# Gate-weight splits placed behind a query tile's convolution, and one chunk's loads placed ahead of the next chunk's, at the seam of two scans

## The chip, the cores and the metric

The kernel runs on one core of one Trainium2 chip. The metric is device time in microseconds (us) for one execution. The profile's engines are PE (matrix products; PEld is its weight load), DVE (elementwise work), ACT (activation functions, scaled copies), POOL (elementwise work, some DMA issue) and SP (DMA issue only).

## The reference

One layer over 4096 rows of width 1024, float32. After an RMS norm, one projection yields the operands of two groups. Group B is a windowed attention. Group A, which matters here, is a matrix-memory recurrence in both directions over 32 chunks of 128 rows with 4 heads of 128:

```python
qk_a = jax.nn.silu(centred_depthwise_conv(qk_a, conv_w, conv_b))
q_a, k_a = jnp.split(qk_a.astype(jnp.float32), 2, axis=-1)
...
h_fwd = mlstm_one_direction(q_a, k_a, v_a, i_f, f_f)
h_bwd = jnp.flip(mlstm_one_direction(jnp.flip(q_a, 1), jnp.flip(k_a, 1), jnp.flip(v_a, 1),
                                     jnp.flip(i_b, 1), jnp.flip(f_b, 1)), 1)
h = jax.nn.sigmoid(o_a.astype(jnp.float32)).reshape(hs) * (h_fwd + h_bwd)
h = h * lax.rsqrt(jnp.mean(h * h, axis=-1, keepdims=True) + EPS)
...
y_a = h.reshape(bsz, seqlen, A_WIDTH) * jax.nn.silu(z_a.astype(jnp.float32))
```

Both groups are joined, projected, added to the input and normed again.

## The kernel before

Every large product is made of three products: each operand is split into a high part (a copy rounded to fp32r, made by ACT) and a low part (the rest, by a subtraction on DVE), and high x low, low x high and high x high are summed. A weight tile's split is the pair L104 (ACT) and L105 (DVE) in `load_split`. Each call of `wgroup` loads and splits one weight block of 1024 x 512 as four tiles j = 0..3, and each tile has two such pairs. `next_weights(0)`, `(1)` and `(2)` make `w3_0` (gate o), `w3_1` (gate z) and `w3_2` (the attention's gate). In the trace their staging tiles are `w_0s`, `w_1s`, `w_2s`; in the listings of order they are `w3_1s2` and so on.

The work has three passes. `pass2` walks blocks b = 7 .. 0 of 512 rows backwards: value projection, then eight key and query tiles m (keys m = 4..7, then queries m = 0..3). Each tile is 24 matmuls (L879), an ACT copy to `U` (L883), a first tap on ACT (L895), four taps on DVE (L897), a tanh on ACT (L899), a closing product on DVE (L900) and a store to DRAM (`k_d`, `q_d`, L902). The four key tiles are transposed (`ktp`, PE L927) into a PSUM buffer of tag "b", which has two buffers; ACT casts it (L929) and DVE subtracts (L930) to give the split key `kt`. The "b" buffers go in turn to ktp 0, ktp 1, ktp 2, the product kv of chunk 3 and head 1, ktp 3, and so on. The products kv (L158 to L160) need `kt` and the weighted values (`wvr` on POOL and DVE L940, cast L942, low part L943); state C follows on DVE (L958) and goes to DRAM.

`pass3` walks chunks n = 0 .. 31 forwards. For each it computes the gates (`op`, `zp`, 24 matmuls each, L1176, in two PSUM buffers of tag "pj" that go in turn to op 0, zp 0, op 1, zp 1; the ACT tanh L1184 reads them out), loads query, key, value and state (`lq`, `lk`, `lv`, `lkf`, `CC`, L1084 and L1064) and two broadcast rows `E` and `W` (L1060), masks E on POOL (L1092), takes its exponential on ACT (L1096), multiplies the scores S (PE L1104) into it (DVE L1106), weighs the query (DVE L1118) and forms the numerators (L1128, L1129). Chunk 0's query comes from DRAM, where block 0's query tiles were stored.

PE's order is written out by hand. On the other engines a list scheduler orders the instructions by its own model of their times; `behind(c, ins)` holds what is issued within it until `ins` has been placed on that same engine. So the seam from pass2's block 0 to pass3's chunk 0 is where the key and query tiles, the splits of `w3_1` and `w3_2`, and the loads of chunks 0 and 1 share ACT, DVE and SP. The staging tiles of `w3_2` also occupy buffers that the loads of CC 0, E 1, W 1 and CC 1 take over: each of those loads waits for a split on DVE.

Of the kernel before, what the change touches and what calls it, by code (L numbers as in the profile page):

```python
# [823 lines left out]
def pass2(c):  # L824
    nc, tc, A = c.nc, c.tc, c.A
    with ExitStack() as es:
# [37 lines left out]
        def qkproj(b, m):  # L864
            w = wk_ if m >= 4 else wq
            h = m % 4
            cs = slice(h * 128, h * 128 + 128)
            parts = ((0, 258), (258, 514)) if b == 7 else ((0, 512),)
            R = {}

            def unit(lo, hi, k, j):
                if lo == 0 and k == 0 and j == 0:
                    R["U"] = wk.tile([128, 516], F32, tag="U", bufs=2, name=f"U{b}_{m}")
                if k == 0 and j == 0:
                    R["p"] = c.ps("pj", [128, 512], f"up{b}_{m}_{lo}")
                up, U = R["p"], R["U"]
                xh, xl = xv(b, k, lo, hi)
                a, x = ((1, xh), (0, xl), (0, xh))[j]
                nc.tensor.matmul(up[:, 0:hi - lo], w[k // 2][:, k % 2, a, cs], x, start=(k == 0 and j == 0),  # L879
                                 stop=(k == KT - 1 and j == 2))  # L880
                if k < KT - 1 or j < 2:
                    return
                nc.scalar.copy(U[:, lo:hi], up[:, 0:hi - lo])  # L883
                if hi != parts[-1][1]:
                    return
                if m == 4:
                    HL[b] = wk.tile([128, 8, 4], F32, tag="hl", bufs=2, name=f"hl{b}")
                if b == 7:
                    nc.gpsimd.memset(U[:, 514:516], 0.0)
                else:  # L890
                    nc.gpsimd.tensor_copy(U[:, 512:516], HL[b + 1][:, m, :])
                nc.gpsimd.tensor_copy(HL[b][:, m, :], U[:, 0:4])
                cm = (h + 4) if m >= 4 else h
                acc = wk.tile([128, 512], F32, tag="qk", bufs=4, name=f"qk{b}_{m}")
                c.ucopy = nc.scalar.activation(acc, U[:, 0:512], AF.Identity, bias=cb[:, cm:cm + 1], scale=cw[:, cm, 0:1])  # L895
                for t in range(1, 5):
                    nc.vector.scalar_tensor_tensor(acc, U[:, t:t + 512], cw[:, cm, t:t + 1], acc, ALU.mult, ALU.add)  # L897
                th = wk.tile([128, 512], F32, tag="th", bufs=1, name=f"th{b}_{m}")
                nc.scalar.activation(th, acc, AF.Tanh)  # L899
                nc.vector.scalar_tensor_tensor(acc, th, 1.0, acc, ALU.add, ALU.mult)  # L900
                dst = c.k_d if m >= 4 else c.q_d
                nc.sync.dma_start(dst[4 * b:4 * b + 4, :, h * 128:h * 128 + 128].rearrange("n p t -> p n t"),  # L902
                                  acc.rearrange("p (n t) -> p n t", n=4))
                if m >= 4:
                    KTS[b, h] = acc

            return [[[(lambda z=z: unit(*z)) for z in [(lo, hi, k, j) for j in range(3)]] for k in range(KT)]
                    for lo, hi in parts]

# [54 lines left out]
        for b in range(7, -1, -1):  # L964
            for pair in () if b == 7 else ((3, 2), (1, 0)):
                vu = [vproj(4 * b + i) for i in pair]
                for k in range(KT):
                    for u in vu[0][3 * k:3 * k + 3] + vu[1][3 * k:3 * k + 3]:
                        u()
            if b == 0:  # L970
                c.next_weights(0)
            for m in range(4, 8):
                for u in flat(qkproj(b, m)):
                    u()
                if b == 7 and m == 6:
                    gate4(c)
                    rnorm(c)
            n3 = 4 * b + 3
            if b < 7:
                weigh(n3)  # L980

            def kvp(n, hh):
                if hh == 0 and n > n3 - 3:
                    weigh(n - 1)
                kvmm(n, hh)

            fill = flat(qkproj(b, 0))
            if b == 7:
                fill.append(cost(0.0, lambda: (gate5(c), weigh(n3))))
            fill += flat(qkproj(b, 1)) + last_two(b)  # L990
            at = [((8, 16, 28, 38)[h] / 96, lambda h=h, b=b: ktp(b, h)) for h in range(NH)]
            if b == 0:
                at.append((37 / 96, lambda: c.next_weights(1)))
            at += [((34 + 62 * (4 * (n3 - n) + hh) / 16) / 96, lambda n=n, hh=hh: kvp(n, hh))
                   for n in range(n3, n3 - 4, -1) for hh in range(NH)]
            place(fill, at)
            if b == 0:
                with behind(c, c.ucopy):
                    c.next_weights(2)
                c.x0 = XB[0]  # L1000

# [34 lines left out]
def pass3(c):  # L1036
    nc, tc, A = c.nc, c.tc, c.A
    with ExitStack() as es:
# [7 lines left out]
        def load(n, names):  # L1046
            r = Ls.setdefault(n, {})
            for nm in names:
                if n >= NCH:
                    continue  # L1050
                if nm in "ew":
                    nme = f"{nm.upper()}{n}"
                    if nm == "e" and n > 1:
                        e = r[nm] = wk.tile([128, 2, NH, 128], F32, tag="e", bufs=3, name=nme)
                    else:
                        e = r[nm] = xtile(c, [128, 2, NH, 128], F32, nme)
                    for d in range(2):
                        m = (c.m_d if nm == "e" else c.w_d)[d, n if d == 0 else NCH - 1 - n].rearrange("h t -> (h t)")
                        with behind(c, TZ.get("x") if nm == "e" and n < 5 else None):
                            nc.sync.dma_start(e[:, d].rearrange("p h t -> p (h t)"), m.partition_broadcast(128))  # L1060
                    continue
                if nm == "cc":
                    t = CCs[n] = xtile(c, [128, NH, 2, 129], F32, f"CC{n}")
                    nc.sync.dma_start(t[:, :, 1, :], c.cb_d[n].rearrange("p (h d) -> p h d", h=NH))  # L1064
                    continue
                if nm == "x":
                    if n == 0:
                        for i in range(2):
                            XS[i] = lambda a, k, i=i: c.x0[k][:, a, 2 + i * 128:130 + i * 128]
                    elif n % 2 == 0:  # L1070
                        xs = []
                        for i in range(2):
                            XS[n + i] = lambda a, k, i=i, xs=xs: xs[k // 2][:, a, k % 2, i * 128:i * 128 + 128]
                        for kk in range(4):
                            t = xtile(c, [128, 2, 2, 256], F32R, f"xs{n}_{kk}")
                            for z in range(2):
                                TZ["x"] = nc.sync.dma_start(f32(t[:, z]), c.xT_d[z, 2 * kk:2 * kk + 2, :, n * 128:n * 128 + 256]
                                                  .rearrange("k p t -> p k t"))
                            xs.append(t)
                    continue  # L1080
                d = {"q": c.q_d, "k": c.k_d, "kf": c.kf_d, "v": c.v_d}[nm]
                w = 129 if nm in ("kf", "v") else 128
                t = r[nm] = wk.tile([128, NH, w], F32, tag="l" + nm, bufs=2, name=f"l{nm}{n}")
                nc.sync.dma_start(t.rearrange("p h d -> p (h d)"), d[n])  # L1084

        def decays(n):
            if n >= NCH:
                return
            e = Ls[n]["e"]
            for d in range(2):  # L1090
                sg = 1 if d == 0 else -1
                nc.gpsimd.affine_select(out=e[:, d], in_=e[:, d], compare_op=ALU.is_ge, fill=BIG, base=0,  # L1092
                                        pattern=[[0, NH], [sg, 128]], channel_multiplier=-sg)
                with behind(c, TZ.get(n - 1)):
                    for h in range(NH):
                        nc.scalar.activation(e[:, d, h, :], e[:, d, h, :], AF.Exp, bias=tmone(c, 0, d, h, n),  # L1096
                                             scale=-1.0)
# [96 lines left out]

        load(0, ("x", "k", "q", "e", "w", "cc", "v", "kf"))
        nc.gpsimd.memset(CCs[0][:, :, 0, :], 0.0)
        load(1, ("e", "w", "cc", "q", "k"))
        decays(0)
        weigh_q(0)
        load(1, ("v", "kf"))  # L1200
# [298 lines left out]
def body(nc, tc, A):  # L1499
    with ExitStack() as es:  # L1500
        c = setup(nc, tc, A, es)
        c.w3, c.w4, c.XR = [], [], {}

        def next_weights(i):
            c.w3.append(wgroup(c, (1536, 2048, 2560)[i], f"w3_{i}"))

        c.next_weights = next_weights
        with tc.manual_schedule(engines={mybir.EngineType.PE}):
# [47 lines left out]
```

## Time and profile before

| | us |
|---|---|
| runs shown: median of 3 | 2211.18 |
| runs shown: lowest, highest | 2203.68, 2211.2 |
| profiled execution, its own time | 2207.95 |
| its span (first to last instruction) | 2206.2 |
| seam, from the last key tiles to S of chunk 0 | about 1155 to 1206 of the span |

| engine | busy us in the span |
|---|---|
| PE | 2164.2 |
| DVE | 1411.1 |
| ACT | 1087.0 |
| POOL | 608.7 |

The mean granted PE clock is 0.994 of full speed. All times of the trace below count from the span's start. A row of the timeline gives start, length, engine, line, operation, output and inputs, and in brackets how long the engine was idle before it and who ended the idle time. The length of a row includes its completion, so the next row can start a little before it ends.

### The profile page before, as it was taken

How to read it: one execution, taken by the hardware profiler on the slowest of the kernel's cores; microseconds unless marked ns; L12 is line 12 of the kernel's file. 1: busy time of each engine (PE TensorE's matmuls, PEld its weight loads, DVE VectorE, ACT ScalarE, POOL GpSimd, SP SyncE). 2: the span in 40 equal slices, each digit the busy share in tenths (PEclk: the TensorE clock that was granted, in tenths of full speed). 3: DMA queues.
4: the chain of work that ended last, by engine and by line, in shares of the span. 5: the costliest groups of instructions: out<-in, count | busy, mean ns of one | idle time of the engine just before them, and what ended most of it. 6: DMA issues, size and time to landing. Idle time of an engine off the chain costs nothing.

```text
span 2206.2 us, 35191 instructions
## 1 busy us (share of the span) xinstructions
PE 2164.2 (98%) x12226; PEld 1877.9 (85%) x12226; DVE 1411.1 (64%) x3092; ACT 1087.0 (49%) x2712; POOL 608.7 (28%) x1059
## 2 busy tenths in 40 slices
PE   8999999999999999999999999999999999999998
PEld 7899999999797888888887888888888888888886
DVE  6677777787765566456667555555554443777776
ACT  6778888877643343334445444444443321333323
POOL 3456565662121211121112212112121111112222
PEclk9999999999999999999999999999999999999999
DMA  8654464432233452344266976777685998667774
GB/s 246 177 171 123 148 172 98 158 114 69 92 98 106 158 163 78 120 159 154 76 193 219 321 220 214 237 240 230 213 254 177 316 359 284 185 181 187 190 196 138
DMA packets 249134, 398.98 MB, mean 181 GB/s; under 512 B 21979, under 2 KB 128475, under 8 KB 248956
## 3 DMA queue, kind: packets, MB, share of 16 engines
q1 hardware_dynamic: 220544, 303.50, 45.5%
q0 software_dynamic: 28176, 92.96, 13.1%
q8 instruction: 96, 1.57, 0.3%
q14 instruction: 82, 0.67, 0.1%
q10 hardware_dynamic: 236, 0.27, 0.0%
HBM read 275.99 MB, written 120.67 MB: 180 GB/s over the span
## 4 chain that ended last, share of the span: by engine, by line
PE 78%; DMA 8%; issue 5%; DVE 5%; ACT 2%; POOL 2%; POOLq 0%; SPq 0%; DVEq 0%; ACTq 0%
PE up L879 15%; PE zp L1176 8%; PE op L1176 8%; PE qp L532 7%; PE v2p L852 7%; DMA xr<-x 5%; PE op L409 4%; PE tp L395 3%; PE sp L367 3%; PE zbp L158 3%; PE zbp L159 3%; PE zbp L160 3%; PE num L1129 3%; PE num L1128 3%; PE kp L468 2%
## 5 line engine op out<-in xcount | busy, mean ns | idle before, releaser
L879 PE MATMUL up<-xb,w 128*128 128x512 f32 x1344 | 338.3, 396 | 0.0
L1343 PE MATMUL o<-wo,yo 128*128 128x512 f32 (+1 forms) x1356 | 312.3, 392 | 0.0
L1343 PEld LDWEIGHTS o<-wo,yo 128*128 128x128 f32 x1356 | 253.2, 188 | 59.2
L879 PEld LDWEIGHTS up<-xb,w 128*128 128x128 f32 x1344 | 243.8, 188 | 47.0
L897 DVE SCALAR_TENSOR_TENSOR qk<-U,cw,qk 128x512 f32<-128x512 f32 x256 | 190.1, 754 | 93.6 <-ACT qk L895 88.8
L532 PE MATMUL qp<-xT,wqb 128*128 128x256 f32 x1536 | 246.2, 290 | 0.1
L532 PEld LDWEIGHTS qp<-xT,wqb 128*128 128x128 f32 x1536 | 217.2, 192 | 8.9 <-DVE xT L450 0.3
L1176 PE MATMUL op<-w,xs 128*128 128x512 f32 x720 | 202.4, 408 | 0.0
L1176 PE MATMUL zp<-w,xs 128*128 128x512 f32 x720 | 188.0, 402 | 0.7 <-DVE z L1186 0.7
L852 PE MATMUL v2p<-w,xb 128*128 128x512 f32 x672 | 158.0, 395 | 1.1 <-DMA xb<-xT_d 1.0
L1176 PEld LDWEIGHTS zp<-w,xs 128*128 128x128 f32 x720 | 130.9, 189 | 27.6 <-DVE z L1186 1.2
L852 PEld LDWEIGHTS v2p<-w,xb 128*128 128x128 f32 x672 | 126.0, 188 | 31.8 <-DMA xb<-xT_d 2.3
L370 DVE CUSTOM_DVE_ANT_0 s<-sp,G 128x320 f32<-128x320 f32 (+1 forms) x256 | 122.6, 480 | 44.3 <-PE sp L367 40.6
L398 DVE TENSOR_TENSOR pt<-tp,pt 128x512 fp32r<-128x512 f32 x188 | 129.2, 687 | 26.3 <-ACT pt L397 25.0
L379 ACT ACTIVATE s<-s,st 128x320 f32<-128x320 f32 (+1 forms) x256 | 139.7, 548 | 11.5 <-DVE st L377 11.1
L1176 PEld LDWEIGHTS op<-w,xs 128*128 128x128 f32 x720 | 126.8, 189 | 21.1
L397 ACT CAST pt<-tp 128x512 fp32r<-128x512 f32 x188 | 110.0, 586 | 63.5 <-PE tp L395 60.2
L1143 ACT ACTIVATE hs<-num,r 128x128 f32<-128x128 f32 x128 | 47.1, 368 | 175.4 <-DVE r L1140 129.3
L409 PE MATMUL op<-pt,v 128*128 128x512 f32 x376 | 121.8, 405 | 10.4 <-DVE ab L422 10.3
L367 PE MATMUL sp<-kk,q 128*128 128x320 f32 (+2 forms) x512 | 119.6, 315 | 4.3 <-DVE st L370 4.2
L395 PE MATMUL tp<-ident,s 128*128 128x128 f32 x752 | 114.2, 275 | 0.2 <-DVE pt L398 0.2
L1166 POOL DMA_DIRECT2D y_d<-ya x32 | 19.4, 607 | 326.0 <-ACT hs L1143 182.9
(274 smaller groups left out, 4529.9 us busy)
## 6 DMA issues: line engine op xcount, KB each, us to landing
xc<-xT_d SPq DMA_DIRECT2D x64, 512.0 KB, 8.2
xs<-xT_d SPq DMA_DIRECT2D x120, 256.0 KB, 6.4
xT_d<-xT POOLq DMA_DIRECT2D x104, 256.0 KB, 5.4
xb<-xT_d SPq DMA_DIRECT2D x48, 514.0 KB, 7.6
E<-m_d SPq DMA_DIRECT2D x64, 256.0 KB, 4.6
W<-w_d SPq DMA_DIRECT2D x64, 256.0 KB, 5.8
y<-y_d SPq DMA_DIRECT2D x32, 512.0 KB, 3.4
out<-xr POOLq DMA_DIRECT2D x31, 512.0 KB, 4.1
```

What stands on the lines that cost most here:

```text
L367: nc.tensor.matmul(sp[:, lo:hi], qt, kk[:, kv, z, col - 128 + lo:col - 128 + hi], start=(z == 0), stop=(z == 1))
L370: nc.vector.tensor_tensor_reduce(out=s[:, lo:hi], in0=sp[:, lo:hi], in1=bias[0][:, kv * 2 + m, lo - 64 * half:hi - 64 * half], op0=ALU.add ...
L379: nc.scalar.activation(ps[g][:, kept(g)], ps[g][:, kept(g)], AF.Exp, bias=ng[:, g:g + 1], accum_out=rs[:, g:g + 1])
L395: nc.tensor.transpose(tp[:, g * 128:(g + 1) * 128], ps[g][:, j * 128:(j + 1) * 128], c.ident)
L398: nc.vector.tensor_sub(pt[:, 1, :], tp, f32(pt[:, 0, :]))
L409: nc.tensor.matmul(op, vt, pt[:, z, :], start=(i == 0 and z == 0), stop=(i == len(js) - 1 and z == 1))
L532: nc.tensor.matmul(qp, wq[k // 2][:, k % 2, w, m * 128:m * 128 + 128], x[k], start=(k == 0 and j == 0), stop=(k == KT - 1 and j == 2))
L852: nc.tensor.matmul(vp, a, wv[k // 2][:, k % 2, m, :], start=(k == 0 and j == 0), stop=(k == KT - 1 and j == 2))
L879: nc.tensor.matmul(up[:, 0:hi - lo], w[k // 2][:, k % 2, a, cs], x, start=(k == 0 and j == 0), stop=(k == KT - 1 and j == 2))
L897: nc.vector.scalar_tensor_tensor(acc, U[:, t:t + 512], cw[:, cm, t:t + 1], acc, ALU.mult, ALU.add)
L1176: nc.tensor.matmul(P[nm], XS[n](a, k), w[:, m, :], start=(k == 0 and j == 0), stop=(k == KT - 1 and j == 2))
L1343: nc.tensor.matmul(p, a[:, z, k, :], w[k // 2][:, k % 2, m, lo:hi], start=k == 0 and z == 1, stop=k == 3 and z == 0 and m == 0)
```

## The change

There are two edits of the order of splits and two of the order of loads. No operation is added or removed.

```diff
-                nc.scalar.activation(th, acc, AF.Tanh)
-                nc.vector.scalar_tensor_tensor(acc, th, 1.0, acc, ALU.add, ALU.mult)
+                c.qth = nc.scalar.activation(th, acc, AF.Tanh)
+                c.qst = nc.vector.scalar_tensor_tensor(acc, th, 1.0, acc, ALU.add, ALU.mult)
...
                 if m >= 4:
                     KTS[b, h] = acc
+                    c.kth, c.kst = c.qth, c.qst
...
-                at.append((37 / 96, lambda: c.next_weights(1)))
+                def w1():
+                    c.next_weights(1, (0, 1))
+                    with behind(c, c.kth), behind(c, c.kst):
+                        c.next_weights(1, (2, 3))
+
+                at.append((37 / 96, w1))
...
-                with behind(c, c.ucopy):
+                with behind(c, c.qth), behind(c, c.qst):
                     c.next_weights(2)
...
-                nc.sync.dma_start(t.rearrange("p h d -> p (h d)"), d[n])
+                TZ[nm, n] = nc.sync.dma_start(t.rearrange("p h d -> p (h d)"), d[n])
...
-                with behind(c, TZ.get(n - 1)):
+                with behind(c, TZ.get(1 if n == 1 else n - 1)):
...
-        load(1, ("e", "w", "cc", "q", "k"))
+        with behind(c, TZ["q", 0]):
+            load(1, ("e", "w", "cc", "q", "k"))
...
-        def next_weights(i):
-            c.w3.append(wgroup(c, (1536, 2048, 2560)[i], f"w3_{i}"))
+        def next_weights(i, js=range(4)):
+            if len(c.w3) == i:
+                c.w3.append([])
+            c.w3[i] += wgroup(c, (1536, 2048, 2560)[i], f"w3_{i}", js=js)
```

In the listings below a tile's name carries its block and number: `qk0_7` is block 0, m = 7 (the last key tile), `qk0_0` the first query tile, `kt0_2` the split of key tile 2, `th0_3` the tanh of the last query tile.

DVE at the last key tile, before, from the splits of w3_1's third tile to the last key tile's closing product:

```order
L105 SCALAR_TENSOR_TENSOR w3_12_13229<-w3_1s2_13230,nw_88,w3_12_13229 128x512 x2
L897 SCALAR_TENSOR_TENSOR qk0_7_13104<-U0_7_13075,cw_7935,qk0_7_13104 128x512
L900 SCALAR_TENSOR_TENSOR qk0_6_13065<-th0_6_13071,qk0_6_13065 128x512
L930 TENSOR_TENSOR kt0_0_13136<-ktp0_0_13131,kt0_0_13136 128x512
L940 TENSOR_TENSOR wvr1_13299<-v2_1_12918,TM_8723 128x4x129
L105 SCALAR_TENSOR_TENSOR w3_13_13236<-w3_1s3_13237,nw_88,w3_13_13236 128x512
L897 SCALAR_TENSOR_TENSOR qk0_7_13104<-U0_7_13075,cw_7935,qk0_7_13104 128x512
L105 SCALAR_TENSOR_TENSOR w3_13_13236<-w3_1s3_13237,nw_88,w3_13_13236 128x512
L930 TENSOR_TENSOR kt0_1_13152<-ktp0_1_13147,kt0_1_13152 128x512
L897 SCALAR_TENSOR_TENSOR qk0_0_13166<-U0_0_13121,cw_7935,qk0_0_13166 128x512
L930 TENSOR_TENSOR kt0_2_13187<-ktp0_2_13182,kt0_2_13187 128x512
L900 SCALAR_TENSOR_TENSOR qk0_7_13104<-th0_7_13110,qk0_7_13104 128x512
```

The same place on DVE with the change, up to the split of key tile 2 (the two rows ahead of it are the first taps of qk0_7 and the closing product of qk0_6):

```order
L931 TENSOR_TENSOR kt0_0_13136<-ktp0_0_13131,kt0_0_13136 128x512
L897 SCALAR_TENSOR_TENSOR qk0_7_13104<-U0_7_13075,cw_7935,qk0_7_13104 128x512
L931 TENSOR_TENSOR kt0_1_13152<-ktp0_1_13147,kt0_1_13152 128x512
L897 SCALAR_TENSOR_TENSOR qk0_7_13104<-U0_7_13075,cw_7935,qk0_7_13104 128x512
L897 SCALAR_TENSOR_TENSOR qk0_0_13166<-U0_0_13121,cw_7935,qk0_0_13166 128x512
L900 SCALAR_TENSOR_TENSOR qk0_7_13104<-th0_7_13110,qk0_7_13104 128x512
L897 SCALAR_TENSOR_TENSOR qk0_0_13166<-U0_0_13121,cw_7935,qk0_0_13166 128x512
L105 SCALAR_TENSOR_TENSOR w3_12_13229<-w3_1s2_13230,nw_88,w3_12_13229 128x512 x2
L897 SCALAR_TENSOR_TENSOR qk0_0_13166<-U0_0_13121,cw_7935,qk0_0_13166 128x512
L105 SCALAR_TENSOR_TENSOR w3_13_13236<-w3_1s3_13237,nw_88,w3_13_13236 128x512 x2
L941 TENSOR_TENSOR wvr1_13299<-v2_1_12918,TM_8723 128x4x129
L931 TENSOR_TENSOR kt0_2_13187<-ktp0_2_13182,kt0_2_13187 128x512
```

The closing product of qk0_7 has moved ahead of the four splits, and kt0_2 has moved behind it, behind two more taps of qk0_0 and behind the splits; on ACT the cast of kt0_2 likewise stands behind the four splits now.

ACT from the last query tile's first tap to the tanh of op 0, before:

```order
L895 ACTIVATE qk0_3_13460<-U0_3_13396,cb_7936,cw_7935 128x512
L104 ACTIVATE w3_20_13470<-w3_2s0_13471,nw_88 128x512 x2
L104 ACTIVATE w3_21_13477<-w3_2s1_13478,nw_88 128x512 x2
L104 ACTIVATE w3_22_13484<-w3_2s2_13485,nw_88 128x512 x2
L104 ACTIVATE w3_23_13491<-w3_2s3_13492,nw_88 128x512 x2
L1096 ACTIVATE E0_13510<-E0_13510,TM_8723 128x128 x8
L899 ACTIVATE th0_3_13466<-qk0_3_13460 128x512
L1184 ACTIVATE o0_13600<-op0_13575 128x512
```

The same stretch of ACT with the change:

```order
L895 ACTIVATE qk0_3_13460<-U0_3_13396,cb_7936,cw_7935 128x512
L1102 ACTIVATE E0_13510<-E0_13510,TM_8723 128x128 x8
L899 ACTIVATE th0_3_13466<-qk0_3_13460 128x512
L104 ACTIVATE w3_20_13470<-w3_2s0_13471,nw_88 128x512 x2
L104 ACTIVATE w3_21_13477<-w3_2s1_13478,nw_88 128x512 x2
L104 ACTIVATE w3_22_13484<-w3_2s2_13485,nw_88 128x512 x2
L104 ACTIVATE w3_23_13491<-w3_2s3_13492,nw_88 128x512 x2
L1190 ACTIVATE o0_13600<-op0_13575 128x512
```

The exponentials of E 0 and th0_3 now stand ahead of the eight splits of w3_2, and the tanh of op 0 directly behind them.

SP's queue from the last query stores but one to chunk 0's key and query, before:

```order
L1060 DMA E0_13510<-m_d_72 128x512 x2
L902 DMA q_d_74<-qk0_2_13380 128x4x128
L1060 DMA W0_13513<-w_d_73 128x512 x2
L1064 DMA CC0_13516<-cb_d_78 128x4x129
L1060 DMA E1_13523<-m_d_72 128x512 x2
L1060 DMA W1_13526<-w_d_73 128x512 x2
L1064 DMA CC1_13529<-cb_d_78 128x4x129
L902 DMA q_d_74<-qk0_3_13460 128x4x128
L1084 DMA lk0_13506<-k_d_75 128x512
L1084 DMA lq0_13508<-q_d_74 128x512
```

The same stretch of SP's queue with the change:

```order
L1066 DMA E0_13510<-m_d_72 128x512
L902 DMA q_d_74<-qk0_2_13380 128x4x128
L1066 DMA E0_13510<-m_d_72 128x512
L1066 DMA W0_13513<-w_d_73 128x512 x2
L902 DMA q_d_74<-qk0_3_13460 128x4x128
L1070 DMA CC0_13516<-cb_d_78 128x4x129
L1090 DMA lk0_13506<-k_d_75 128x512
L1090 DMA lq0_13508<-q_d_74 128x512
L1090 DMA lv0_13518<-v_d_77 128x516
L1090 DMA lkf0_13520<-kf_d_76 128x516
L1066 DMA E1_13523<-m_d_72 128x512 x2
```

The store of the last query tile no longer has E 1, W 1 and CC 1 ahead of it; these five loads now follow chunk 0's four. PE's order is the same in both. On POOL only the wvr of chunk 1 moves, behind two small copies. Outside the seam the lists agree, but for a few rows of chunks 2 to 4 that change places with a neighbour.

## The prediction

> **What bounds the kernel now.** I read the page's busy times first, then PE's waits, then the chain that ended last through the seam. PE's row and its waits at the seam:
>
> ```profile
> PE 2164.2 (98%) x12226; PEld 1877.9 (85%) x12226; DVE 1411.1 (64%) x3092; ACT 1087.0 (49%) x2712; POOL 608.7 (28%) x1059
> ```
>
> ```profile
> PE S L1104 <- DMA lq<-q_d: 1.4, 1, 1.4
> PE ktp L927 <- DVE qk L900: 1.1, 1, 1.1
> ...
> PE kv L158 <- DVE kt L930: 0.4, 1, 0.4
> ```
>
> PE is busy for 98% of the span, so only what makes PE wait moves the time. (A wait's row gives total us, times, longest.) In the whole seam PE waits three times, 1.4 + 1.1 + 0.4 = 2.9 us together, 0.13% of the run. This is all that the change can win. The chain shows what ends the two larger waits:
>
> ```profile
> 1167.45 0.60 DVE kt L930
> 1168.05 0.61 DVE qk L900
> 1168.80 0.63 PE ktp L927 x4
> ...
> 1198.97 4.26 DMA q_d<-qk
> 1203.37 2.58 DMA lq<-q_d
> 1206.08 1.13 PE S L1104 x8
> ```
>
> The fourth key transposition waits for the last key tile's closing product on DVE. S of chunk 0 waits for the last query tile, which is stored (4.26 us) and loaded again (2.58 us).
>
> **The first edit: two tiles of w3_1 behind the last key tile.** Rows of PE, DVE, ACT and POOL at this place:
>
> ```profile
> 1160.60 3.03 PE L879 MATMUL up<-xb,w 128*128 128x512 f32 x12
> 1163.66 0.65 PE L927 MATMUL ktp<-ident,qk 128*128 128x128 f32 x4
> ...
> 1167.31 0.40 PE L879 MATMUL up<-xb,w 128*128 128x512 f32 x1
> ...
> 1169.96 0.28 PE L158 MATMUL kv<-wvh,kt 128*128 128x258 f32 x1
> ```
>
> ```profile
> 1157.87 1.54 DVE L897 SCALAR_TENSOR_TENSOR qk<-U,cw,qk 128x512 f32<-128x512 f32 x2 [0.17 <-POOL hl L892]
> 1159.46 1.41 DVE L105 SCALAR_TENSOR_TENSOR w<-w_1s,nw,w 128x512 fp32r<-128x512 f32 x2
> 1160.79 0.75 DVE L897 SCALAR_TENSOR_TENSOR qk<-U,cw,qk 128x512 f32<-128x512 f32 x1
> 1161.45 1.55 DVE L900 SCALAR_TENSOR_TENSOR qk<-th,qk 128x512 f32<-128x512 f32 x1
> 1162.92 0.68 DVE L930 TENSOR_TENSOR kt<-ktp,kt 128x512 fp32r<-128x512 f32 x1
> 1163.53 0.68 DVE L940 TENSOR_TENSOR wvr<-v,TM 128x516 f32<-128x516 f32 x1
> ...
> 1166.72 0.73 DVE L897 SCALAR_TENSOR_TENSOR qk<-U,cw,qk 128x512 f32<-128x512 f32 x1
> 1167.38 0.67 DVE L930 TENSOR_TENSOR kt<-ktp,kt 128x512 fp32r<-128x512 f32 x1
> ...
> 1173.08 0.68 DVE L940 TENSOR_TENSOR wvr<-v,TM 128x516 f32<-128x516 f32 x1
> ```
>
> ```profile
> 1163.04 0.58 ACT L883 COPY U<-up 128x512 f32<-128x512 f32 x1
> 1163.66 0.81 ACT L895 ACTIVATE qk<-U,cb,cw 128x512 f32<-128x512 f32 x1
> ```
>
> ```profile
> 1160.96 1.50 POOL L940 TENSOR_TENSOR wvr<-v,TM 128x516 f32<-128x516 f32 x1 [2.94 <-DVE w L105]
> ...
> 1171.86 2.82 POOL L940 TENSOR_TENSOR wvr<-v,TM 128x516 f32<-128x516 f32 x1 [5.62 <-PE kv L160]
> ```
>
> From start to start a tap (1166.72 to 1167.38) or a split (1.41 less one length of 0.75) costs DVE 0.66 us, a subtraction 0.60 (1162.92 to 1163.53), a closing product 0.61 by the chain.
>
> The fourth transposition needs more than the closing product. Its PSUM buffer is that of the third, so DVE must have subtracted kt0_2 as well. That PE really waits for such a buffer shows in the third one: it starts at 1163.66, 0.2 us after twelve matmuls of 0.23 us from 1160.60 are through, when kt0_0, whose buffer it takes, is done (1162.92 + 0.68). Before the change kt0_2 was done at 1168.05 and hid behind the closing product. Now it comes later:
>
> - From 1157.87 DVE has two taps (to 1159.4), closing product, kt0_0, tap, kt0_1 and tap, whose inputs are ready (kt0_1's cast comes at about 1161.4): done at 1162.8.
> - The next row in its list, the first tap of qk0_0, waits for ACT. PE has finished that tile 8 matmuls after 1160.60, about 1162.6; the copy takes 0.58 and the first tap 0.81, with small gaps 1164.1. DVE stands idle for some 1.3 us with the closing product queued behind.
> - From 1164.2: tap, closing product, tap, two splits, tap, two splits, wvr: 7 x 0.66 + 0.61 + 0.60 = 5.8. Then kt0_2 with 0.67: 1170.7. ACT's cast of it, behind four splits of its own, is through by 1167.8 and doesn't bind.
>
> So the transposition starts at about 1170.8 in place of 1168.80: the named wait goes, but kt0_2 is late by more. **Term one: +2.0 us.** Bounds: if the buffer did not bind, the product that needs kt0_2 itself would wait; it stood at 1169.96, so +0.8. If DVE loses 0.9 to POOL's wvr of chunk 1, which now runs beside the splits (a closing product took 1.55 in place of 0.67 while POOL's wvr ran from 1160.96), +2.9. If DVE's idle 1.3 us did not come about, +0.7.
>
> [...]
>
> **The second edit: w3_2's splits behind the last query tile.** I keep the times of before; all of it shifts with term one. Rows:
>
> ```profile
> 1188.60 0.82 ACT L895 ACTIVATE qk<-U,cb,cw 128x512 f32<-128x512 f32 x1
> 1189.33 5.00 ACT L104 ACTIVATE w<-w_2s,nw 128x512 fp32r<-128x512 f32 x8
> 1194.24 2.44 ACT L1096 ACTIVATE E<-E,TM 128x128 f32<-128x128 f32 x8
> 1197.01 0.63 ACT L899 ACTIVATE th<-qk 128x512 f32<-128x512 f32 x1 [0.34 <-DVE qk L897]
> 1197.55 0.58 ACT L1184 ACTIVATE o<-op 128x512 f32<-128x512 f32 x1
> ```
>
> ```profile
> 1191.99 1.80 POOL L1092 TENSOR_SCALAR_AFFINE_SELECT E<-E 128x512 f32<-128x512 f32 x2 [3.17 <-DMA E<-m_d]
> ```
>
> ```profile
> 1186.87 0.84 SPq L1060 DMA_DIRECT2D E<-m_d  x2
> ```
>
> ```profile
> 1198.89 5.75 PE L1176 MATMUL op<-w,xb 128*128 128x512 f32 x24
> 1206.08 1.13 PE L1104 MATMUL S<-lq,lk 128*128 128x128 f32 x8 [1.45 <-DMA lq<-q_d]
> ```
>
> Before, ACT ran the eight splits while E 0 was still landing. Now E 0's exponentials come first, and E 0 lands no earlier: its load waits for the last kv product and was issued at 1186.87, POOL could mask it from 1191.99. So ACT is idle from 1189.4 to 1192.9, when the first mask is done (1.80 / 2). Eight exponentials 2.44: 1195.3. The tanh of the last query tile: 1195.9. Eight splits 5.00: 1200.9. Only then the tanh of op 0, 0.58: 1201.5. This frees the PSUM buffer that op 1 takes, and PE wants to begin op 1 at 1198.89, when zp 0 is through. Before, this tanh was done at 1198.1, in time by 0.8. Now **PE waits about 2.5 us for ACT**.
>
> The last query tile is indeed earlier: closing product at 1196.6 in place of 1198.9, store 4.26, load 2.58, there at 1203.6. Op 1 then ends at 1201.4 + 5.75 = 1207.2, S starts at once, and its wait of 1.45 is gone. S stands at 1207.2 against 1206.08. **Term two: +1.1 us.** Bounds: if E 0 came as early as ACT was free, the same work as before would end op 0's tanh at about 1198.1, PE would wait for nothing and the term would be -1.45. If the second half of E 0, now issued behind the store of query tile 2, landed 2 us later than its twin, +3.1.
>
> **The loads.** With chunk 1's loads behind chunk 0's, SP meets CC 0 first, which waits for w3_2's first split on DVE (about 1197.9), and then lk 0; lq 0 follows the store. E 1, W 1 and CC 1 are issued from about 1204, some 8 us later than E 1 was. Nothing needs them before the scores of chunk 1 are multiplied, which follows S of chunk 0 by about 9 us, so I cost this at nothing; POOL's mask and ACT's exponentials of E 1 fall into ACT's idle time after op 1. The exponentials of E 1 move behind the tanh of op 1: nothing. POOL's own moves: its wvr of chunk 1 runs 7 us later, and kv of chunk 1 is another 8 us off: nothing.
>
> **Sum.** +2.0 + 1.1 = +3.1 us against the profiled execution's own 2207.95 (span 2206.2 and 1.75 around it): 2211.05. The four executions known (2203.68, 2207.95, 2211.18, 2211.2) have the median 2209.57, 1.6 below the median of the three runs shown; on that middle the forecast is **2212.7 us**.
>
> **Rivals.**
>
> Both waits go as the diff has it, and nothing takes their place: -2.9 us, 2206.7. For it: the closing products do move ahead of eight splits. Against it: DVE's and ACT's lists, which put kt0_2 and the tanh of op 0 behind the same work. It would need kt0_2 done by 1167.2, 3.5 us before my count.
>
> One of the two new waits fails to come. Term one alone with S freed: +2.0 - 1.45 = +0.6; term two alone: -1.5 + 1.1 = -0.4. About 2209.7.
>
> Slower still: the wait at the transposition lowers PE's clock. PE reaches it at about 1167.2 and leaves at 1170.8, idle 3.6 us. What such gaps did in this trace, after a wait of 4.25 us at 71 us and in the window of S's 1.45 us:
>
> ```profile
> 71.03 0.87 PE L367 MATMUL sp<-kk,q 128*128 128x320 f32 x2 [4.25 <-DVE st L370]
> ```
>
> ```profile
> 70.00:72.00 2.00, 0.97 (x4) 1.00 (x5) 1.84 (x5) 1.94 (x5) 2.00 (x3) 0.50 0.72 295
> ...
> 76.00:78.00 2.00, 2.00 (x18) 1.91 (x16) 0.78 (x4) 1.95 (x6) 0.48 (x2) 1.00 0.00 0
> ```
>
> ```profile
> 1204.00:1206.00 2.00, 0.64 (x3) 0.19 (x1) 0.00 (x0) 0.60 (x1) 0.00 (x0) 1.00 0.82 240
> ```
>
> (The figure after POOL's is the granted clock.) After 4.25 us idle PE ran at 0.50 until about 76, after 1.45 us at 1.00. So the point lies between. At half speed for up to 5 us PE loses up to 2.5 us: +5.6, 2215.2. [...]
>
> **How the numbers follow.** Forecast 0.45, lower clock 0.25, one new wait only 0.17, both waits gone 0.08, something else 0.05. The executions of before spread over 2203.68 to 2211.2, 3.8 to either side of their middle; with this about the cases from 2206.7 to 2215.2, leaving out a tenth at each end, the range is 2205.0 to 2218.5. A change of 0.5%, 11 us, is about what a measurement of this kernel can tell from none. No case reaches it: faster 0.02, same 0.95, slower 0.03.
>
> **What would show it.** Term one: a wait of PE at the fourth transposition released by DVE's subtraction L931, 3 to 4 us long, with DVE idle before the first tap of qk0_0; wrong if PE has no wait there. Term two: a wait of op 1 (L1182) for the tanh of op 0 (L1190) of 2 to 3 us, ACT idle for over 3 us before E 0's exponentials, and no wait at S. The lower clock: a granted clock under 1.00 just behind the transposition. The forecast is wrong if PE's waits between 1155 and 1210 sum to less than 3 us or to more than 9.

## The result, and the profile after

| | before | after |
|---|---|---|
| median of 12 runs each, us | 2208.78 | 2215.24 |
| ratio of the times, 95% interval | | 1.0035 (1.0027 to 1.0042) |
| profiled execution, its own time, us | 2207.95 | 2214.36 |
| its span, us | 2206.2 | 2212.6 |
| PE busy, us | 2164.2 | 2163.2 |

The change costs 0.35%, that is 7.7 us (6.0 to 9.3 us), under the 0.5% that the prediction drew as its line. One of the twelve runs before took 2649.85 us, in a slower state, and the ratio leaves it out. PE does the same work; in the seam it waits longer and does part of the work at half clock. PE's waits in the seam after the change (total us, times, longest):

```profile
PE ktp L928 <- DVE kt L931: 4.6, 1, 4.6
PE op L1182 <- ACT o L1190: 4.2, 1, 4.2
```

The seam's two waits of before, 1.08 us at the transposition and 1.45 us at S, have become two large ones, at the two places that the prediction named. (The third that the prediction counts, 0.4 us of a kv product, is not in the seam: it starts at 646.40 us before and at 644.43 us after.) S waits no more. PE's rows through the seam (start, us, operation, count; in brackets the idle time before it):

```profile
1156.02 0.60 PE L928 MATMUL ktp<-ident,qk 128*128 128x128 f32 x4
...
1164.78 0.39 PE L879 MATMUL up<-xb,w 128*128 128x512 f32 x1
1169.78 0.71 PE L928 MATMUL ktp<-ident,qk 128*128 128x128 f32 x4 [4.61 <-DVE kt L931]
1170.19 1.58 PE L879 MATMUL up<-xb,w 128*128 128x512 f32 x3
...
1190.28 5.73 PE L1182 MATMUL op<-w,xb 128*128 128x512 f32 x24
1195.85 5.75 PE L1182 MATMUL zp<-w,xb 128*128 128x512 f32 x24
1205.83 8.27 PE L1182 MATMUL op<-w,xb 128*128 128x512 f32 x24 [4.22 <-ACT o L1190]
1213.94 1.05 PE L1110 MATMUL S<-lq,lk 128*128 128x128 f32 x8
```

Behind both waits the same matmuls take longer: three at L879 1.58 us in place of 0.94, the 24 of op 1 8.27 us in place of 5.75. The windows show why (stretch, its length, busy time of PE, PEld, DVE, ACT and POOL, then the granted clock, the DMA share and GB/s):

```profile
1165.00:1169.00 4.00, 0.17 (x1) 0.00 (x0) 4.00 (x6) 1.08 (x4) 1.49 (x1) 1.00 0.15 44
1169.00:1171.00 2.00, 1.22 (x6) 1.13 (x7) 1.90 (x5) 1.53 (x2) 0.00 (x0) 0.81 0.00 0
1171.00:1173.00 2.00, 2.00 (x7) 1.68 (x7) 1.54 (x3) 0.91 (x3) 0.00 (x0) 0.50 0.00 0
...
1205.00:1207.00 2.00, 1.17 (x3) 0.98 (x4) 1.42 (x3) 1.25 (x3) 0.00 (x0) 0.50 1.02 323
1207.00:1209.00 2.00, 2.00 (x7) 1.52 (x6) 1.47 (x2) 0.00 (x0) 0.00 (x0) 0.50 1.06 346
1209.00:1211.00 2.00, 2.00 (x6) 1.61 (x5) 0.35 (x1) 0.00 (x0) 0.64 (x1) 0.50 1.02 279
```

PE was granted half its clock behind each wait. Whole spans scatter by several us from work ahead of the seam (the first key transposition of the last block starts between 1154.26 and 1159.06 us in the thirteen traces of this case), so from here on the seam is measured on its own, as the time between PE's rows: from the first key transposition of the last block (T0) to the fourth (T3), to op 0, to op 1, to S of chunk 0 and to S of chunk 2. There is one trace of each kernel.

| us | T0 to T3 | T3 to op 0 | op 0 to op 1 | op 1 to S 0 | T0 to S 0 | T0 to S 2 |
|---|---|---|---|---|---|---|
| before | 10.85 | 18.93 | 11.16 | 7.19 | 48.13 | 72.94 |
| after | 13.76 | 20.50 | 15.55 | 8.11 | 57.92 | 82.05 |
| difference | +2.91 | +1.57 | +4.39 | +0.92 | +9.79 | +9.11 |

The spans differ by less, 6.4 us, because this execution reached T0 1.93 us earlier (1156.02 against 1157.95) and spent 0.8 us less behind S of chunk 2. The ratio's 7.7 agrees with the 9.11 within its interval.

DVE and POOL ahead of the fourth transposition, after:

```profile
1162.39 0.75 DVE L897 SCALAR_TENSOR_TENSOR qk<-U,cw,qk 128x512 f32<-128x512 f32 x1 [1.47 <-POOL U L891]
1163.06 0.69 DVE L900 SCALAR_TENSOR_TENSOR qk<-th,qk 128x512 f32<-128x512 f32 x1
...
1164.33 1.41 DVE L105 SCALAR_TENSOR_TENSOR w<-w_1s,nw,w 128x512 fp32r<-128x512 f32 x2
...
1166.31 2.20 DVE L105 SCALAR_TENSOR_TENSOR w<-w_1s,nw,w 128x512 fp32r<-128x512 f32 x2
1168.43 0.68 DVE L941 TENSOR_TENSOR wvr<-v,TM 128x516 f32<-128x516 f32 x1
1169.04 0.68 DVE L931 TENSOR_TENSOR kt<-ktp,kt 128x512 fp32r<-128x512 f32 x1
```

```profile
1165.81 1.49 POOL L941 TENSOR_TENSOR wvr<-v,TM 128x516 f32<-128x516 f32 x1 [4.00 <-DVE w L105]
```

The closing product, for which PE had waited before, is there at 1163.7. The subtraction of kt 0_2 ends at 1169.7, behind four splits, of which the last two took 0.79 us longer than the first two while POOL's wvr ran. The bracket of 1.47 us names POOL's small copy, but that row ends at 1161.8; ACT's first tap, for which the prediction had DVE wait, ends at 1162.30, just ahead of DVE's row.

ACT, POOL and SP ahead of op 1, after:

```profile
1194.71 1.29 ACT L1102 ACTIVATE E<-E,TM 128x128 f32<-128x128 f32 x4 [2.16 <-POOL E L1098]
1198.57 1.29 ACT L1102 ACTIVATE E<-E,TM 128x128 f32<-128x128 f32 x4 [2.56 <-POOL E L1098]
1199.76 0.62 ACT L899 ACTIVATE th<-qk 128x512 f32<-128x512 f32 x1
1200.28 5.01 ACT L104 ACTIVATE w<-w_2s,nw 128x512 fp32r<-128x512 f32 x8
1205.20 0.58 ACT L1190 ACTIVATE o<-op 128x512 f32<-128x512 f32 x1
```

```profile
1193.78 0.90 POOL L1098 TENSOR_SCALAR_AFFINE_SELECT E<-E 128x512 f32<-128x512 f32 x1 [1.54 <-DMA E<-m_d]
1197.90 0.64 POOL L1098 TENSOR_SCALAR_AFFINE_SELECT E<-E 128x512 f32<-128x512 f32 x1 [3.22 <-DMA W<-w_d]
```

```profile
1189.42 0.34 SPq L1066 DMA_DIRECT2D E<-m_d  x1
1191.64 0.37 SPq L902 DMA_DIRECT2D q_d<-qk  x1
1192.06 0.50 SPq L1066 DMA_DIRECT2D E<-m_d  x1
```

The store of query tile 2 stands between the two halves of E 0, and its data were not ready, so the second half was issued 2.6 us behind the first. ACT, which meets E 0's exponentials ahead of the splits, waited for each half, and op 0's tanh came at 1205.20. (The bracket of POOL's second row names W 0's load, which the mask does not read; it was issued right behind that half.)

### The profile page after: what moved, and what is told of

Same layout as the page of the kernel before. It is cut to its first block, busy times and chain, and to the rows that moved or that the text cites. A ratio compares the mean times of both kernels' runs of the same rounds, so it can differ in the third digit from the quotient of the medians.

```text
span 2212.6 us, 35188 instructions
## 1 busy us (share of the span) xinstructions
PE 2163.2 (98%) x12226; PEld 1876.8 (85%) x12226; DVE 1413.0 (64%) x3092; ACT 1090.1 (49%) x2712; POOL 604.5 (27%) x1059
## 3 DMA queue, kind: packets, MB, share of 16 engines
q8 instruction: 96, 1.57, 0.3%
## 5 line engine op out<-in xcount | busy, mean ns | idle before, releaser
L879 PE MATMUL up<-xb,w 128*128 128x512 f32 x1344 | 339.6, 397 | 0.0
L879 PEld LDWEIGHTS up<-xb,w 128*128 128x128 f32 x1344 | 244.6, 189 | 47.2
L409 PE MATMUL op<-pt,v 128*128 128x512 f32 x376 | 121.4, 404 | 10.6 <-DVE ab L422 10.5
L367 PE MATMUL sp<-kk,q 128*128 128x320 f32 (+2 forms) x512 | 119.5, 315 | 5.8 <-DVE st L370 5.8
```

The costliest lines, as they stand in the source:

```text
L367: nc.tensor.matmul(sp[:, lo:hi], qt, kk[:, kv, z, col - 128 + lo:col - 128 + hi], start=(z == 0), stop=(z == 1))
L409: nc.tensor.matmul(op, vt, pt[:, z, :], start=(i == 0 and z == 0), stop=(i == len(js) - 1 and z == 1))
```

## The experiments

The theory: (1) the first edit delays the fourth transposition through kt 0_2; (2) the second edit delays op 1 through op 0's tanh, and the late half of E 0 adds to it; (3) each wait is long enough to halve PE's clock behind it. Ratios are against the kernel before, run beside it; legs are those of the table above.

### The parts by themselves

Only the first edit: in the changed kernel,

```diff
-                with behind(c, c.qth), behind(c, c.qst):
+                with behind(c, c.ucopy):
                     c.next_weights(2)
...
-                with behind(c, TZ.get(1 if n == 1 else n - 1)):
+                with behind(c, TZ.get(n - 1)):
...
-        with behind(c, TZ["q", 0]):
-            load(1, ("e", "w", "cc", "q", "k"))
+        load(1, ("e", "w", "cc", "q", "k"))
```

> Only the first edit: two tiles of w3_1 behind the last key tile; w3_2's splits and the loads stand as before the change. Theory (the first edit costs by itself a wait at the fourth transposition and half clock behind it, and it also turns the second half of E 0 behind the store of query tile 2): from the first to the fourth transposition 13.5 to 14 us against 10.85 before; wait there 4 to 5 us released by DVE's subtraction, clock under 0.8 just behind it; op 1 waits for op 0's tanh for 1 to 2 us and S still waits for the last query tile; +5 to +8 us against the kernel before. Rival (only the wait itself costs, the lower clock is a matter of how matmuls are recorded): +2 to +3.

Measured 1.0027 (1.0017 to 1.0038). Legs 13.75, 20.55, 11.16, 7.95; T0 to S 2 77.81, 4.87 more than before. The wait and the clock came as the theory has them. Op 1 did not wait at all, which the theory had wrong. S still waited, as expected, and longer than before:

```profile
1210.33 1.13 PE L1110 MATMUL S<-lq,lk 128*128 128x128 f32 x8 [2.21 <-DMA lq<-q_d]
```

Only the second edit, with the loads and E 1's exponentials:

```diff
-                    with behind(c, c.kth), behind(c, c.kst):
-                        c.next_weights(1, (2, 3))
+                    c.next_weights(1, (2, 3))
```

> Only the second edit with the order of the loads and of E 1's exponentials; w3_1 as before the change. Theory (the second edit alone has both halves of E 0 in front of the store of query tile 2, so op 0's tanh is late by only some 2.5 us): fourth transposition as before (wait 1.1), op 1 waits 2 to 3 us, clock there stays 1.00, S does not wait; +0.5 to +1.5 us against the kernel before. Rival (the wait of op 1 comes from the second edit whatever the first does): op 1 waits 4 us or more at half clock, +4.5 to +6.

Measured 0.9999 (0.9990 to 1.0008). PE's row of op 1:

```profile
1198.68 5.84 PE L1181 MATMUL op<-w,xb 128*128 128x512 f32 x24 [1.83 <-ACT o L1189]
```

Op 1 waits 1.83 us, a little less than expected, at full clock; S does not wait; T0 to S 2 is 72.98, 0.04 more than before. What the second edit with its loads costs at op 1 (+1.99) it wins back at S (-1.51) and in the next two chunks. The two runs cost 4.87 and 0.04 us, both edits together 9.11: **the loss comes from the first edit, and from what it does to the second.** Here both halves of E 0 are issued together, at 1184.68, ahead of the store of query tile 2; with the first edit that store stands between them.

Only the loads and E 1's exponentials (that edit above, and w3_2's splits behind c.ucopy again):

> Only the order of the loads (chunk 1's behind lq 0) and of E 1's exponentials; both weight edits undone. Theory (the loads cost nothing): same three small waits as before at the seam, S still waits about 1.4 us; within 0.7 us of the kernel before. Rival (part of the loss is that chunk 1's tiles land 8 us later): a wait of PE in chunk 1 or 2, +2 us or more.

Measured 1.0008 (0.9999 to 1.0016). Here the theory fell. Two of PE's waits:

```profile
PE op L1181 <- DMA xs<-xT_d: 2.0, 1, 2.0
...
PE yp L1168 <- DVE hs L1161: 1.5, 2, 1.2
```

No wait at S any more, with every split where it had been: T0 to S 0 is 45.97, 2.2 less than before, of which 1.60 is in the leg from op 1 to S 0 and 0.58 ahead of T3, where the order is that of before. But op of chunk 2 then waits 2.0 us for its rows, the transposed heads of chunk 0 wait 1.5, and T0 to S 2 is 74.78, 1.84 more. The new order of the loads alone frees S, and it comes with a wait in chunk 2. That the changed kernel escapes this wait because its S comes 12 us later is not shown: the run of the second edit has the same order of loads, its S comes only 2.6 us later, and it has no such wait.

### The first wait

Both held tiles of w3_1 also behind kt 0_2's subtraction:

```diff
-            nc.vector.tensor_sub(kt[:, 1], tp, f32(kt[:, 0]))
+            c.kts = nc.vector.tensor_sub(kt[:, 1], tp, f32(kt[:, 0]))
...
-                    with behind(c, c.kth), behind(c, c.kst):
+                    with behind(c, c.kth), behind(c, c.kst), behind(c, c.kts):
```

> The changed kernel with the two held tiles of w3_1 also behind the third key tile's subtraction (kt 0_2). Theory (the fourth transposition waits because kt 0_2 stands behind four splits): its wait falls under 1 us and the clock stays 1.00 there; both halves of E 0 come in front of the store of query tile 2, op 1 waits 2 to 3 us in place of 4.2 and keeps its clock; 0 to +1.5 us against the kernel before, 6 us or more better than the changed one. Rival (the splits only move the wait to the next tile, the product with kt 0_3 or S): some other wait of 2 us or more between the fourth transposition and op 0, no better than +4 against the kernel before.

Measured 1.0032 (1.0019 to 1.0044). PE's rows:

```profile
1167.28 0.66 PE L928 MATMUL ktp<-ident,qk 128*128 128x128 f32 x4 [1.46 <-DVE kt L931]
...
1172.45 0.39 PE L158 MATMUL kv<-wvh,kt 128*128 128x258 f32 x1 [2.52 <-DVE kt L931]
...
1205.46 8.55 PE L1182 MATMUL op<-w,xb 128*128 128x512 f32 x24 [3.56 <-ACT o L1190]
```

The wait at the transposition falls to 1.46 us (under 1 us was expected), so kt 0_2 was its cause. The rival holds for the rest: the splits now stand ahead of kt 0_3, and the product that needs it waits 2.52 us, with the clock at 0.50 soon behind it. T3 to op 0 grows to 23.29. Op 1 waits 3.56 us although both halves of E 0 were issued together: they took 6.7 us to land. T0 to S 2 is 81.33, only 0.7 less than with the change.

One of the two tiles behind kt 0_2 (the same edit, for tile 3 alone):

> The changed kernel with one of the two held tiles of w3_1 also behind the third key tile's subtraction. Theory (two splits fewer in front of kt 0_2, 1.4 to 2.2 us): wait at the fourth transposition 2.4 to 3.2 us, and, as a gap of 2.52 us did in the run that moved both tiles, it still lowers the clock behind it for 2 to 4 us; 1.5 to 2.5 us better than the changed kernel. [...]

Measured 1.0022 (1.0013 to 1.0032). PE's row, and the windows behind it:

```profile
1168.54 0.66 PE L928 MATMUL ktp<-ident,qk 128*128 128x128 f32 x4 [2.48 <-DVE kt L931]
```

```profile
1168.00:1170.00 2.00, 1.46 (x10) 1.33 (x11) 2.00 (x4) 0.59 (x1) 0.80 (x1) 1.00 0.00 0
1170.00:1172.00 2.00, 1.33 (x8) 0.82 (x7) 2.00 (x5) 1.63 (x3) 0.00 (x0) 1.00 0.00 0
```

The wait is as long as expected, but the clock, expected to fall, stays at 1.00 behind it. T0 to S 2 is 78.18, 3.9 us less than with the change, where 1.5 to 2.5 was expected; 2.7 of it is won up to op 0, and the rest comes behind op 0, where op 1 waits 2.71 us.

### The second wait and the clock

The splits of the last tile, or of the last two tiles, of w3_2 behind op 0's tanh, their loads where they were:

```diff
-                    c.next_weights(2)
+                    c.next_weights(2, (0, 1, 2))
+                c.late = [None] * 3 + [stage(c, win_src(c, 2 * j, 2, 2560, 512), 2, 512, f"w3_2s{j}")
+                                     for j in (3,)]
...
-        for u in p0 + p1[:24]:
+        for u in p0[:24]:
+            u()
+        with behind(c, TZ[0]):
+            c.next_weights(2, (3,), c.late)
+        for u in p0[24:] + p1[:24]:
             u()
...
-        def next_weights(i, js=range(4)):
+        def next_weights(i, js=range(4), sts=(None,) * 4):
...
-            c.w3[i] += wgroup(c, (1536, 2048, 2560)[i], f"w3_{i}", js=js)
+            c.w3[i] += wgroup(c, (1536, 2048, 2560)[i], f"w3_{i}", sts=sts, js=js)
```

> The changed kernel with the splits of one of w3_2's four tiles behind op 0's tanh (its load stays where it was). Theory (PE waits at op 1 for op 0's tanh behind those splits, each tile 1.25 us of ACT; a gap of 3 us is still long enough to lower the clock): op 1 waits 2.7 to 3.2 us in place of 4.2, op 1's 24 matmuls still take over 7 us; 1 to 2 us better than the changed kernel. [...]

> The changed kernel with the splits of two of w3_2's four tiles behind op 0's tanh. Theory: op 1 waits 1.4 to 2 us, clock 1.00, its 24 matmuls take 5.75; from the first transposition to S 57.9 - 2.5 - 2.5 = 52.9 us, unless S or the burst of loads of chunks 1 and 2 then makes PE wait; 3 to 5 us better than the changed kernel. Rival (the lower clock comes from something else in this place, such as the DMA load): the 24 matmuls stay over 7 us.

One tile: 1.0030 (1.0019 to 1.0042). PE's row and two windows:

```profile
1203.82 7.41 PE L1184 MATMUL op<-w,xb 128*128 128x512 f32 x24 [2.09 <-ACT o L1192]
```

```profile
1204.00:1206.00 2.00, 2.00 (x7) 1.54 (x8) 1.73 (x3) 1.48 (x3) 0.00 (x0) 0.64 1.07 337
1206.00:1208.00 2.00, 2.00 (x6) 1.58 (x5) 0.86 (x1) 0.00 (x0) 0.00 (x0) 0.50 0.96 321
```

A gap of only 2.09 us, shorter than the 2.7 to 3.2 expected, still lowered the clock; T0 to S 2 is 79.77. Two tiles: 1.0031 (1.0019 to 1.0043). Op 1 waits 0.2 us (leg 11.35) and runs 5.82; T0 to S 0 is 52.20, near the 52.9 expected. Of the 5.7 us won there half is given back: the waits of the next chunks show

```profile
PE num L1137 <- DVE E L1114: 1.5, 1, 1.5
```

E 1, loaded and masked late, now binds; T0 to S 2 is 79.14.

The same gap with PE kept busy: twelve more matmuls, whose results nobody reads, between zp 0 and op 1.

```diff
+        dm = c.ps("y", [128, 512], "dm")
+        for i in range(12):
+            nc.tensor.matmul(dm, XS[0](0, i % 8), wo[0][:, 0, 0, :], start=True, stop=True)
```

> The changed kernel with twelve matmuls (0.23 us each, into a PSUM bank that is free there and that nobody reads) between zp 0 and op 1, where PE waits for op 0's tanh. Theory (PE's own idle time lowers its clock): op 1 begins when it did before, behind an idle of some 1.5 us, and its 24 matmuls take 5.75 us in place of 8.27; 2 to 2.8 us better than the changed kernel, though PE does more. Rival (the clock falls with what runs beside, ACT's splits or the loads): op 1 still takes over 7 us and the time is that of the changed kernel.

Measured 1.0028 (1.0017 to 1.0040). PE's rows:

```profile
1200.27 2.99 PE L1215 MATMUL dm<-w,xb 128*128 128x512 f32 x12
1203.63 5.85 PE L1182 MATMUL op<-w,xb 128*128 128x512 f32 x24 [0.38 <-ACT o L1190]
```

Op 1 began 1.0 us earlier than with the change (op 0 to op 1 is 14.52), with the same splits and loads beside it, and ran its 24 matmuls in 5.85 us, with the granted clock at 1.00: op 1 to S 0 is 5.69 in place of 8.11. That PE's own idleness lowers its clock is **shown**: with the gap filled, but for 0.38 us, the clock stays at 1.00 where it was 0.50, although ACT, DVE and the loads do what they did. S 0 stands at 55.06, 2.9 us earlier. Of this 2.4 us is the clock and 1.0 us the earlier start, against 0.6 more between T3 and op 0. The earlier start is not the matmuls' doing: op 1 waits for op 0's tanh on ACT here too, 0.38 us. The total against before does not separate from the changed kernel's; the legs do.

The store of query tile 2 out of the way of E 0:

```diff
-                nc.sync.dma_start(dst[4 * b:4 * b + 4, ...
+                (nc.gpsimd if b == 0 and m == 2 else nc.sync).dma_start(dst[4 * b:4 * b + 4, ...
```

> The changed kernel with the store of query tile 2 issued by POOL, so that on SP nothing stands between the two halves of E 0. Theory (that store holds E 0's second half by 2.6 us, and the exponentials behind it hold op 0's tanh): op 1 waits 1.8 to 2.9 us in place of 4.2; its clock may fall or not (gaps of 2.09 and 2.71 us lowered it in earlier runs, 1.83 did not); from the first transposition to S of chunk 2 77.3 to 80.2 us against 82.05 in the changed kernel. Rival (E 0 lands late for its own reasons, as in the run with kt 0_2 first): op 1 waits 3.5 us or more, 81 to 82 us.

Measured 1.0026 (1.0016 to 1.0037). PE's row:

```profile
1206.93 7.12 PE L1182 MATMUL op<-w,xb 128*128 128x512 f32 x24 [2.53 <-ACT o L1190]
```

The wait falls from 4.22 to 2.53 us, T0 to S 2 to 78.99. So the late half of E 0 was 1.7 us of the wait between these two traces; as the run with the filled gap shows, op 1's start can move by 1 us with the same splits and loads (14.52 against 15.55 from op 0). In the three runs that issue both halves together and have all splits of w3_2 behind E 0's exponentials, op 1's wait follows the time from E 0's issue to its first exponential: 5.6 us and a wait of 1.83 (second edit alone), 6.3 and 2.53 (this run), 7.3 and 3.56 (both tiles behind kt 0_2).

### A version to beat both

The kernel before, with only CC 1, lq 1 and lk 1 behind lq 0, and E 1's exponentials where the change has them:

```diff
-        load(1, ("e", "w", "cc", "q", "k"))
+        load(1, ("e", "w"))
+        with behind(c, TZ["q", 0]):
+            load(1, ("cc", "q", "k"))
```

> A version meant to beat both: the kernel before with only CC 1, lq 1 and lk 1 behind lq 0; E 1 and W 1 stay ahead, w_3's splits as before the change. Theory (S waited because chunk 1's loads shared the transfers with the last query tile's store and load, and what came too late in the loads-only run were the loads of chunk 2 behind the whole of chunk 1's): S waits less than 1 us, no wait of over 1 us in chunks 1 and 2; from the first transposition to S of chunk 2 71.5 to 72.9 us against 72.94; 0 to 1.4 us better than before. Rival (any load put off comes too late): as the loads-only run, 74 to 75 us.

Measured 0.9990 (0.9982 to 0.9999). Its waits:

```profile
PE num L1134 <- DVE E L1111: 0.7, 1, 0.7
...
PE S L1109 <- DMA lq<-q_d: 0.3, 1, 0.3
```

S waits 0.3 us; the next chunk waits 0.7 for E 1's scores. T0 to S 2 is 72.70, 0.24 less than before. The interval just leaves out no change, but the seam itself accounts for 0.24 of some 2 us, and the leg T0 to T3 alone differs by up to 0.58 us between traces with the same order there, so I would not call the gain settled. It beats the changed kernel.

The same with the fourth transposition four units later in the filling (place 42 of 96 in place of 38, last block only):

> As the run before, and the fourth key transposition four units of 96 later in the filling, where the last key tile's closing product is done. Theory: PE's wait of 1.1 us there goes; 70.4 to 71.9 us from the first transposition to S of chunk 2, 1 to 2.5 us better than before. Rival (kt 0_3 is then late, the product that needs it waits instead): as the run before, within 0.3 us.

Measured 1.0002 (0.9993 to 1.0011). The transposition waits no more, and the product with kt 0_3 waits 1.26 us: the rival. T0 to S 2 is 73.15, 0.45 more than in the run before, where the rival allowed 0.3.

## Why the prediction was right, and where it fell short

The forecast was +3.1 us and 2212.7 us; the median came to 2215.24, inside the range of 2205.0 to 2218.5, and the size class (within 0.5%, on the slower side) came true. The places, the causes and the direction were right; the amount was not: the ratio gives +7.7, the seam paid +9.1 us. The time misses by only 2.5 us, in part by luck: it started from 2209.57, and the twelve runs before have 2208.78. The prediction's own sign, waits of 3 to 9 us in all between 1155 and 1210, was met narrowly, with 4.61 + 4.22 = 8.83. Where the rest came from, step by step:

- **Term one, +2.0 forecast, +2.91 measured** (T0 to T3, and the same 13.75 to 13.76 in all six kernels with that order). The mechanism is the one given: closing product early, kt 0_2 behind four splits, DVE idle 1.47 us for the first tap. The size is off by the choice between zero and the upper bound for POOL's wvr beside the splits: the bound, +2.9, is what came, 0.79 us of it lost by the splits and 0.17 in the longer idle time. The length of POOL's row does not give what DVE loses beside it: the row took 1.49 us here, of which the first 0.58 (1165.81 to 1166.39) lies beside a tap on DVE that took its usual 0.74; in the run with both tiles behind kt 0_2 POOL's wvr took 1.05 us, and the two splits beside it lost 0.81. Before, beside the closing product, POOL's wvr took 1.50 us and DVE lost 0.87; beside the next wvr, 2.82 us from 1171.86, DVE's own share took its usual 0.68 and a closing product 1.28, 0.59 more than the usual 0.69.
- **Term two's wait, 2.5 us forecast, 4.22 measured.** Again the place and the cause are right, and again the bound came close (the second half 2 us late, a wait of 4.5): the second half of E 0 came late. The step that failed is that query tile 2's data would be there by the time SP met their store. Moving that store away gave 2.53 us, what was forecast.
- **S's wait of 1.45 gone: right, for a reason that was incomplete.** The prediction put it on the earlier closing product. The run of the loads, with every split where it had been, removed it too: the store of the last query tile lands 2.3 us after its issue with the change and 2.4 in the run of the loads, and took 4.3 us before. Whether the earlier closing product would have done it without the loads, no run shows. In the run of the second edit alone this gain pays for most of the wait at op 1.
- **The loads at nothing: right in the changed kernel, wrong as a reason.** The prediction asked when chunk 1 needs its loads; in the run of the loads it is the rows of chunk 2, issued behind them, for which PE waits 1.96 us.
- **The lower clock, held as a rival for one gap, came at both.** Behind the transposition it cost 1.57 us (T3 to op 0). At op 1 it cost 2.42: the leg from op 1 to S 0 is 8.11, and 5.69 in the run with the filled gap. Together 4.0 us, the largest single miss. Failed is the step from rows of 1.45 us (no drop) and 4.25 us (drop) to a chance of only 0.25 for a drop behind a gap of 3.6; the 0.25 was the author's estimate, and no row showed it. The trace of before had nearer rows, and they spoke for the drop: a gap of 3.49 us, shorter than the 3.6 forecast, and one of 2.25 us, each with the clock near half behind it.

```profile
497.66 0.73 PE L409 MATMUL op<-pt,v 128*128 128x512 f32 x2 [3.49 <-DVE ab L422]
```

```profile
499.00:501.00 2.00, 2.00 (x12) 2.00 (x11) 1.45 (x5) 0.48 (x2) 1.00 (x4) 0.52 0.22 80
```

```profile
27.64 0.55 PE L445 MATMUL xtp<-ident,x 128*128 128x128 f32 x3 [2.25 <-DVE x L196]
```

```profile
28.00:30.00 2.00, 2.00 (x12) 2.00 (x11) 0.69 (x1) 0.59 (x1) 0.00 (x0) 0.51 0.71 160
```

Adding up to S 0: 2.91 + 1.57 + 4.39 + 0.92 = 9.79. Of this 0.7 comes back by S of chunk 2, most of it at the transposed heads of chunk 0 (`yp`), whose four matmuls take 1.09 us before and 0.60 after.

The rivals with both waits gone or one of them gone fell; the most that the change could win was the 2.5 us of the two waits in the seam, not 2.9. The lower clock at T3 alone would have given 2215.2, and the median came to 2215.24, but that is chance: its +5.6 held one clock drop, the kernel has two.

## What to carry to other kernels

When an instruction is moved ahead of weight splits, list what the splits are now ahead of: here they moved from in front of the closing product to in front of kt 0_2, then, in a repair, to in front of kt 0_3, and each time PE waited for the next tile (4.61 us, then 2.52). In these traces the granted clock fell to half behind some of PE's waits from 1.77 us on and behind every one of 2.52 us or more in the table below, and op 1's 24 matmuls then took up to 8.65 us in place of 5.75, so price such a wait with up to 2.9 us more. Matmuls that compute nothing can be cheaper than the idle time that they fill: with twelve of them ahead of op 1 the leg from op 1 to S 0 took 5.69 us in place of 8.11. A load split in two is as late as its second half (E 0's was issued 2.6 us behind the first), so look at what stands between them in the queue.

## What was not expected of the hardware

The clock drop does not follow the length of the gap alone. Idle time ahead of PE, and the lowest granted clock behind it; the rows with a line number and a time are far ahead of the seam, at instructions that the change does not touch, read from the traces of before and after:

| gap, us | where | clock behind it |
|---|---|---|
| 1.63, 1.75 | L409, after: 551.87 and 561.89 | 1.00 |
| 1.68 | L159 at about 640 us, before and after | 1.00, both |
| 1.77 | L409, before: 552.86 | 0.50 |
| 1.83 | op 1, second edit alone | 1.00 |
| 1.96 | op of chunk 2, loads alone | 1.00 |
| 2.09 | op 1, one tile later | 0.50 |
| 2.21 | S 0, first edit alone | 1.00 |
| 2.25 | L445 at about 27.6 us, before and after | 0.50 before, 1.00 after |
| 2.48 | T3, one tile behind kt 0_2 | 1.00 |
| 2.52 | product with kt 0_3, 1.46 idle 4 us ahead of it | 0.50 |
| 2.53 | op 1, store on POOL | 0.55, mean of 2 us |
| 2.71 | op 1, one tile behind kt 0_2 | 0.50 |
| 3.49 to 5.75 | L409 at about 497 us, L367 at about 71 us, before and after | 0.50, all |
| 3.56 to 4.61 | op 1 and T3, all seen | 0.50 |

From 1.77 to 2.48 us it went either way. The gap at L445 is the plainest case, for the change touches nothing near it: before it ends in half clock (shown above), after the change in full clock.

```profile
27.65 0.55 PE L445 MATMUL xtp<-ident,x 128*128 128x128 f32 x3 [2.25 <-DVE x L196]
```

```profile
28.00:30.00 2.00, 2.00 (x19) 2.00 (x18) 0.69 (x1) 0.59 (x1) 0.03 (x1) 1.00 0.82 163
```

Why the same gap of 2.25 us ended at 0.51 in one execution and at 1.00 in another, no run shows. The six kernels with a gap of 4.6 us at T3 lost between 1.3 and 2.5 us behind it (T3 to op 0 from 20.26 to 21.43 us against 18.93).

The time that one 256 KB load took to land differed by up to 3.3 us: the halves of E 0 and E 1 took 3.4 to 5.3 us from issue to landing in the kernel before, those of E 0 6.7 us in the run with kt 0_2 first, and op 1's wait there was longer for it (3.56 us, against 2.53 in the run with the store on POOL).
